# In the second feed-forward, every fourth weight unit gets its low part from an accumulating DMA instead of a subtraction

## The chip, the cores and the metric

The kernel runs on one core of one Trainium2 chip. The metric is device time in microseconds (us) of that core. The kernel before took 2350.02 us in the median of two runs (2349.10 and 2350.94). One core has a matrix engine (TensorE, PE in the profile, with its weight loads as PEld), a vector engine (VectorE, DVE), a scalar engine (ScalarE, ACT), a general engine (GpSimd, POOL), and a sync engine (SP) that in this kernel issues DMAs only. Sixteen DMA engines move data between HBM, the large memory, and SBUF, the on-chip memory of 128 partitions. TensorE adds up its products in PSUM banks.

## The reference, cut to what matters

A decoder layer on 256 tokens of width 2048 in float32: a feed-forward, a token mixer (windowed attention beside a recurrence), cross attention into a fixed memory, a second feed-forward and a last norm. The change lies in the second feed-forward, whose width is 5632:

```python
def swiglu(h, w_gate, w_up, w_down):
    return (jax.nn.silu(h @ w_gate) * (h @ w_up)) @ w_down

x = x + 0.5 * swiglu(rms_norm(x, ffn2_norm[l]), ffn2_w_gate[l], ffn2_w_up[l], ffn2_w_down[l])
return rms_norm(x, final_norm)
```

## The kernel before, in words

All products with weights follow one plan (`weight_plan`). A product takes up to 16 row chunks of 128 rows and 512 columns of a weight matrix, and both halves of the tokens; its two sums lie in two PSUM banks `acc`, of which there are three. It is worked off in **units** of two row chunks, that is 256 x 512 float32 weights, 512 KB.

float32 is had from a narrower type, float32r, with two parts: a value is a high part, rounded to float32r, plus a low part, what is left. Activations are kept as such pairs. Weights come raw and are split on the way, once a unit:

- `load` (L274): SP issues the DMA of raw weights (L287). In the feed-forwards one DMA brings two units, 1 MB, into a tile `raw2` with four buffers, up to eight units ahead of the one multiplied. SP can issue it when the unit pair that had the buffer before is read for the last time.
- `divide` (L291): ACT casts the raw unit to float32r, `hi` (L299), and DVE subtracts it from the raw weights, `lo` (L300). Both tiles have three buffers, so unit u+2 can be cast when the products of unit u-1 are done. `divide` is called two units ahead (`AHEAD`).
- `multiply` (L331): for each row chunk and each half of the tokens three products, high by high (L336), high activations by low weights (L337), low activations by high weights (L338): twelve a unit.

The order in which the program issues instructions on each engine is that of the Python calls, a little rearranged by a scheduler, and each engine works off its own queue in order. Between the products stand short steps of other work: transposes of the gated values (L347), their split, and in the second feed-forward a reload of `x` and of the last norm's gain by POOL (L1153, L1155). At the end of each of the last four down products ACT squares the result (L1165) and POOL multiplies it by the gain (L1167).

The second feed-forward has 264 units: three groups of gate and up products (8 units each) and of down products (8, 8 and 6 units each, four products a group).

Of the kernel before, what the change touches and what calls it, by code (L numbers as in the profile page):

```python
# [9 lines left out]
AF = mybir.ActivationFunctionType  # L10
# [17 lines left out]
KU = 2  # L28
# The decayed query-side factors carry 2^-40, the masks and the carried state 2^40: no product
# of a later key with an earlier query, which the masks remove, can overflow.  # L30
UP, DOWN = 2.0**40, 2.0**-40
GROUPS = ((0, 4), (4, 4), (8, 3))
N4 = 20
# Weight units whose split, and whose load, runs ahead of the one that is multiplied.
AHEAD, LOADED = 2, 4
# Products before the mixer, and before the second feed-forward.
EDGES = (34, 71)


class Act:  # L40
    """Activations with features on partitions, as two float32r parts that add up to them."""

# [8 lines left out]
class Interleave:  # L51
    """Short steps of other work, traced between the steps of the weight products."""

# [35 lines left out]
def weight_plan(a):  # L89
    """Every product with a weight matrix in its order: matrix, row chunk, chunks, column, columns."""  # L90
    w = {n: v[0] for n, v in a.items() if "_w_" in n or n.startswith("w_")}
    yield from feed_forward_plan(w["ffn1_w_gate"], w["ffn1_w_up"], w["ffn1_w_down"])
    w_in = w["w_in"]
    cols = [0, 512, ATTN_W]
    for c in cols:
        yield w_in, 0, KD, c, 512
    yield w_in, 0, KD, C_RW + 3 * RW, 288
    for h in range(2):
        yield w_in, 0, KD, C_RW + RW + h * 512, 512
    for n in range(4):  # L100
        yield w_in, 0, KD, C_GATE + n * 512, 512
        yield w["w_proj_attn"], 0, 8, n * 512, 512
    for h in range(2):
        yield w_in, 0, KD, C_RW + h * 512, 512
        yield w_in, 0, KD, C_RW + 2 * RW + h * 512, 512
    for n in range(4):
        yield w_in, 0, KD, C_GATE + D + n * 512, 512
    for n in range(4):
        yield w["w_proj_rwkv"], 0, 8, n * 512, 512
    for n in range(4):  # L110
        yield w["w_out"], 0, KD, n * 512, 512
    yield w["w_cross_kv"], 0, KD, 0, 512
    yield w["w_cross_q"], 0, KD, 0, 512
    yield w["w_cross_kv"], 0, KD, 512, 512
    for n in range(4):
        yield w["w_cross_o"], 0, 4, n * 512, 512
    yield from feed_forward_plan(w["ffn2_w_gate"], w["ffn2_w_up"], w["ffn2_w_down"])
# [3 lines left out]
def decoder_layer(ctx: ExitStack, tc: tile.TileContext, a: dict, out: bass.AP):  # L121
# [18 lines left out]
    def f32(x):  # L140
        return x.bitcast(F32)
# [17 lines left out]

# [1 line left out]
    ones = cpool.tile([P, P], F32, name="ones")  # L161
# [9 lines left out]
    select(ident[:], ones[:], [[-1, P]], ALU.is_equal, 0.0, 0, 1)  # L171
    # attention bias: [previous block | current block], rows are queries
    abias = cpool.tile([P, 2, P], F32, name="abias")
    pool.memset(abias[:], 0.0)
    select(abias[:, 0, :], abias[:, 0, :], [[1, P]], ALU.is_gt, NEG, 0, -1)
    select(abias[:, 1, :], abias[:, 1, :], [[-1, P]], ALU.is_ge, NEG, 0, 1)
    # masks with the source step on partitions and the later step along the row
    ups = cpool.tile([P, P], F32, name="ups")
# [4 lines left out]
    select(mask3[:, 2, :], ups[:], [[1, P]], ALU.is_ge, 0.0, 0, -1)  # L183
    # with the later step on partitions
    mask_l = cpool.tile([P, P], F32, name="mask_l")
# [20 lines left out]

# [1 line left out]
    def row_vectors(rows, name, queue):  # L208
        """The vectors, and what fills them once their rows are there."""
        n = len(rows)  # L210
        r = cpool.tile([n, P], F32, name=name + "_r")
        at = 0
        while at < n:
            src, lo = rows[at]
            m = 1
            while at + m < n and rows[at + m][0] is src and rows[at + m][1] == lo + m * P:
                m += 1
            queue.dma_start(
                r[at : at + m, :], src[lo : lo + m * P].rearrange("(c p) -> c p", p=P)
            )  # L220
            at += m
        v = cpool.tile([P, n], F32, name=name)

        def fill():
            t = tr()
            pe.transpose(t[:, :n], r[:], ident[:n, :n])
            return act.copy(v[:], t[:, :n])

        return v, fill
# [36 lines left out]

# [1 line left out]
    plan = list(weight_plan(a))  # L268
# [5 lines left out]
    def load(u):  # L274
        """In the feed-forwards two units at once, into the pool of that phase."""
        if u >= len(units) or u in raws:
# [14 lines left out]
    def divide(u):  # L291
        if u >= len(units) or u in parts:
            return
        n, raw = units[u][3], raws[u]
        hi = wp.tile([P, KU, n], F32R, tag="hi", name="hi")
        lo = wp.tile([P, KU, n], F32R, tag="lo", name="lo")
        for s in (slice(0, 1), slice(1, 2)) if u == 0 else (slice(0, KU),):
            with tc.issue_after(first.ins) if u < AHEAD else nullcontext():
                act.copy(hi[:, s], raw[:, s])  # L299
            dve.tensor_tensor(lo[:, s], raw[:, s], f32(hi[:, s]), ALU.subtract)  # L300
        parts[u] = hi, lo
# [10 lines left out]
    def product(x: Act, w, skew=False):  # L312
        """Rows of tokens: two [128, n] banks of x.T @ (the next columns of w)."""
        pw, _, nk, _, n = plan[at["product"]]
# [25 lines left out]
    def feat(tok, cols):  # L340
        """Token rows [128, 2, n] -> at up to two column offsets [128, 2, T] with features on
        partitions."""
        b = tr()
# [6 lines left out]
    def split(x: Act, c, n, src):  # L350
        """src (float32, PSUM or SBUF) -> chunks c to c + n of x."""
        act.copy(x.at(0, c, n), src)  # L352
        dve.tensor_tensor(x.at(1, c, n), src, f32(x.at(0, c, n)), ALU.subtract)
        x.done |= set(range(c, c + n))

# [1 line left out]
    class Norm:  # L357
# [8 lines left out]
        def block(self, n, src):  # L366
            """Steps for column block n of 512, src [128, 2, 512]; the last one ends the sums."""
            for h in range(2):
# [28 lines left out]

# [1 line left out]
    def feed_forward(sp, x, norm: Norm, wg, wu, wd, done, last=False):  # L399
# [41 lines left out]

    # ==== feed-forward 1 ====
    with tc.tile_pool(name="f1", bufs=1, reuse_waits="tile") as sp:
# [28 lines left out]

    # ==== token mixer and cross attention ====
    with tc.tile_pool(name="mx", bufs=1, reuse_waits="tile") as sp:
# [17 lines left out]

        # -- attention: a group of heads and a block of queries at a time --
        def to_features(tok, dst, name):
# [14 lines left out]
        def keys_values():  # L509
            # keys of each of the four heads on both halves of the partitions  # L510
            b = feat(tok_kv, C4[:2])
# [88 lines left out]

        # -- RWKV: columns with token shift, features on partitions --
        def shifted(tok, cols, mus, outs, name):
# [35 lines left out]
        def decay_and_rate():  # L638
# [28 lines left out]
            for h in range(2):  # L667
# [15 lines left out]
                act.activation(dec[h][:], dec[h][:], AF.Exp, scale=-DECAY)  # L683
                # decay from the middle of a chunk to each step, after that to the step before it
                ee.append(t4("ee", (P, 8, P + 1)))
# [10 lines left out]
        def removal_keys(h):  # L696
# [39 lines left out]
            pool.tensor_tensor(aa[h][:], kt[h][:], ei[:], ALU.mult)  # L736
            # products of the removal keys of later with those of earlier steps: L
            for c in range(2):
# [20 lines left out]

        # (1 - D)^-1 of the 32-step diagonal blocks, one block per partition  # L760
        def substitute():
# [27 lines left out]

        # -- the attention branch, gated --  # L790
        for n in range(4):
# [8 lines left out]

        # -- RWKV: receptances and values --
        rt, vtok, bv = [], [], []
# [15 lines left out]
        def values(h):  # L818
# [3 lines left out]
            for c in range(2):  # L822
                b = tr()
                # the recurrence keeps, and the group norm wants, values less their mean in a head
                for j in range(4):
# [16 lines left out]

        # -- RWKV: the two chunks of a pair of heads --
        xb = {}
# [121 lines left out]

        # -- group norm, bonus, gate, for two pairs --
        yr = Act([], [], 4)
# [53 lines left out]

        # -- the gate of the RWKV branch --
        for n in range(4):
# [5 lines left out]

        # -- merge and project out --
        mt = act_tiles("mt", 4)
# [38 lines left out]

        # -- cross attention --
        km, vm, qc = t4("km"), t4("vm", (P, 2, 512)), t4("qc")
# [68 lines left out]

    # ==== feed-forward 2 and the last norm ====
    with tc.tile_pool(name="f2", bufs=1, reuse_waits="tile") as sp:
# [69 lines left out]
```

## Time and profile before

| | |
|---|---|
| median of the runs | 2350.02 us (2349.10 to 2350.94) |
| span of the profiled execution | 2345.8 us; the runs' median is 4.2 us longer, what lies around the span |
| TensorE busy | 2323.1 us, 99% of the span |
| DVE, ACT, POOL busy | 1256.9, 1075.6 and 130.3 us |
| low parts on DVE (L300) | 769, 1223 ns each in the mean |
| casts on ACT (L299) | 769, 1044 ns each in the mean |
| moved by DMA | 432.71 MB, 184 GB/s over the span |
| granted clock of TensorE, mean | 0.999 |

An engine's busy time is the sum of its instructions' durations. The chain of waits is followed back from the last instruction: at each step to what released it, or to the instruction ahead of it on its engine. In a row of the timeline stand the start in us, the duration in us, engine, line, operation, output and inputs, and in brackets how long the engine was idle before it and what released it. The matmul rows overlap, as matmuls are pipelined: one is 0.39 us long, and the next starts about 0.23 us after it.

### The profile page before, as it was taken

What the parts mean: (1) busy time and instruction counts of PE and PEld (TensorE: products, weight loads), DVE (VectorE), ACT (ScalarE), POOL (GpSimd) and SP (SyncE); (2) the same over time, 40 slices, a digit from 0 to 9 for tenths busy, and PEclk for the clock granted to TensorE, in tenths of its full rate; (3) what the DMA queues carried; (4) which work ended last, traced back from release to release, by engine and by line L of the source; (5) the groups of instructions that cost most, each with busy time, mean ns of one, the idle gap of its engine ahead of it and who ended that gap; (6) DMA issues with size and microseconds to landing.
All of it is one profiled execution on the core that took longest, in us unless ns stands there. A gap on an engine that the chain in (4) does not pass through costs nothing.

```text
span 2345.8 us, 27378 instructions
## 1 busy us (share of the span) xinstructions
PE 2323.1 (99%) x10869; PEld 1897.3 (81%) x10869; DVE 1256.9 (54%) x1393; ACT 1075.6 (46%) x1425; POOL 130.3 (6%) x192
## 2 busy tenths in 40 slices
PE   8999999999999999999999999999999999999998
PEld 7888888888888877888888878888888888888886
DVE  5544444544555477795444456555545544544554
ACT  5443344433445477444344546455443344434444
POOL 1000000000000000201220030001000000000001
PEclk9999999999999999999999999999999999999999
DMA  8555556655554644676432576648555556555653
GB/s 288 182 194 183 194 185 192 190 187 188 188 188 145 177 128 146 211 224 200 118 99 84 182 246 218 192 161 290 186 193 184 187 190 195 183 190 187 197 180 126
DMA packets 219856, 432.71 MB, mean 184 GB/s; under 512 B 14267, under 2 KB 17040, under 8 KB 219728
## 3 DMA queue, kind: packets, MB, share of 16 engines
q1 hardware_dynamic: 211520, 405.58, 54.3%
q0 software_dynamic: 8176, 25.38, 3.4%
q8 instruction: 85, 1.39, 0.2%
q14 instruction: 43, 0.35, 0.0%
q10 hardware_dynamic: 32, 0.01, 0.0%
HBM read 417.56 MB, written 13.11 MB: 184 GB/s over the span
## 4 chain that ended last, share of the span: by engine, by line
PE 93%; issue 4%; DVE 1%; ACT 1%; DMA 1%; POOL 0%; SPq 0%; POOLq 0%; ACTq 0%
PE acc L336 28%; PE acc L338 28%; PE acc L337 28%; PE tr L347 2%; PE mm L925 1%; PE tr L893 1%; DMA raw<-in_ffn_w_gate_dram 0%; ACT hi L299 0%; PE mm L536 0%; POOL ml L1047 0%; PE tr L908 0%; PE tr L912 0%; PE tr L995 0%; DVE lo L300 0%; PE tr L575 0%
## 5 line engine op out<-in xcount | busy, mean ns | idle before, releaser
L300 DVE TENSOR_TENSOR lo<-raw,hi 128x1024 fp32r<-128x1024 f32 (+1 forms) x769 | 940.2, 1223 | 981.5 <-ACT hi L299 980.7
L299 ACT CAST hi<-raw 128x1024 fp32r<-128x1024 f32 (+1 forms) x769 | 802.5, 1044 | 1084.1 <-PE acc L338 1040.8
L336 PE MATMUL acc<-hi,xhi 128*128 128x512 f32 (+1 forms) x2016 | 798.6, 396 | 0.8 <-ACT xhi L373 0.5
L337 PE MATMUL acc<-lo,xhi 128*128 128x512 f32 (+1 forms) x2016 | 784.7, 389 | 0.3 <-DVE lo L300 0.3
L338 PE MATMUL acc<-hi,xlo 128*128 128x512 f32 (+1 forms) x2016 | 784.8, 389 | 0.0
L336 PEld LDWEIGHTS acc<-hi,xhi 128*128 128x128 f32 x2016 | 379.4, 188 | 81.1 <-issue 3.4
L337 PEld LDWEIGHTS acc<-lo,xhi 128*128 128x128 f32 x2016 | 379.4, 188 | 79.0 <-issue 3.3
L338 PEld LDWEIGHTS acc<-hi,xlo 128*128 128x128 f32 x2016 | 378.7, 188 | 79.3 <-issue 1.0
L336 PE MATMUL acc<-hi,hhi 128*128 128x512 f32 x704 | 280.6, 399 | 0.0
L338 PE MATMUL acc<-hi,hlo 128*128 128x512 f32 x704 | 279.1, 396 | 0.0
L337 PE MATMUL acc<-lo,hhi 128*128 128x512 f32 x704 | 279.0, 396 | 0.0
L338 PEld LDWEIGHTS acc<-hi,hlo 128*128 128x128 f32 x704 | 132.6, 188 | 32.3
L337 PEld LDWEIGHTS acc<-lo,hhi 128*128 128x128 f32 x704 | 132.7, 188 | 31.5
L336 PEld LDWEIGHTS acc<-hi,hhi 128*128 128x128 f32 x704 | 132.6, 188 | 31.4
L336 PE MATMUL acc<-hi,mthi 128*128 128x512 f32 x128 | 51.7, 404 | 0.0
L338 PE MATMUL acc<-hi,mtlo 128*128 128x512 f32 x128 | 50.6, 395 | 0.0
L337 PE MATMUL acc<-lo,mthi 128*128 128x512 f32 x128 | 50.4, 394 | 0.0
L1167 POOL TENSOR_TENSOR x<-x,fin 128x512 f32<-128x512 f32 x6 | 8.9, 1497 | 704.0 <-ACT junk L1165 704.0
L465 POOL DMA_DIRECT2D x1d<-x x4 | 3.0, 744 | 717.9 <-DVE x L427 717.9
L415 ACT ACTIVATE hb<-acc,rs 128x512 f32<-128x512 f32 x44 | 30.2, 691 | 19.6 <-PE acc L338 19.6
L352 ACT CAST hhi<-tr 128x512 fp32r<-128x512 f32 x44 | 25.7, 585 | 16.7 <-PE tr L347 16.7
L373 ACT ACTIVATE xhi<-tr,gains 128x256 fp32r<-128x256 f32 x48 | 22.0, 472 | 22.1 <-DVE xlo L374 16.2
(288 smaller groups left out, 1640.8 us busy)
## 6 DMA issues: line engine op xcount, KB each, us to landing
raw<-in_ffn_w_up_dram SPq DMA_DIRECT2D x88, 1024.0 KB, 5.2
raw<-in_ffn_w_down_dram SPq DMA_DIRECT2D x88, 1024.0 KB, 5.1
raw<-in_ffn_w_gate_dram SPq DMA_DIRECT2D x86, 1024.0 KB, 5.2
raw<-in_w_in_dram SPq DMA_DIRECT2D x136, 512.0 KB, 3.7
raw<-in_w_out_dram SPq DMA_DIRECT2D x32, 512.0 KB, 4.3
raw<-in_w_proj_attn_dram SPq DMA_DIRECT2D x16, 512.0 KB, 3.8
raw<-in_w_proj_rwkv_dram SPq DMA_DIRECT2D x16, 512.0 KB, 6.4
raw<-in_w_cross_kv_dram SPq DMA_DIRECT2D x16, 512.0 KB, 3.6
```

What stands on the lines that cost most here:

```text
L299: act.copy(hi[:, s], raw[:, s])
L300: dve.tensor_tensor(lo[:, s], raw[:, s], f32(hi[:, s]), ALU.subtract)
L336: pe.matmul(o, xh, hi[:, i, :], start=k + i == 0, stop=False)
L337: pe.matmul(o, xh, lo[:, i, :], start=False, stop=False)
L338: pe.matmul(o, xl, hi[:, i, :], start=False, stop=k + i == nk - 1)
L347: pe.transpose(b[:, o : o + P], tok[:, t, col : col + P], ident[:])
L352: act.copy(x.at(0, c, n), src)
L373: last = act.activation(self.x.at(0, c), b[:, j, :], AF.Copy, scale=g)
L415: act.activation(hb[:, t, :], pg[t][:], AF.Silu, scale=norm.r[t])
L893: pe.matmul(b[e][:, m * P : (m + 1) * P], x1[r, j, cs_], x2[r, j, cs_], start=True, stop=True,)
L925: pe.matmul(vb[:, (o + e) * P : (o + e + 1) * P], lhs(e), rhs[:], start=first and e == 0, stop=True, **ek,)
L1167: pool.tensor_tensor(xs, xs, fin[:, n * 512 : (n + 1) * 512], ALU.mult)
```

## The change

From the 41st unit of the second feed-forward on (`u >= ends[1] + 40`), every fourth unit (`u % 4 == 1`) forms its low part in another way. ACT casts the high part as before, then writes the negated high part into the low tile. POOL then issues a DMA that adds the raw weights onto that tile. Every second time the raw weights are read from HBM once more, otherwise from the raw tile in SBUF. The other units are unchanged, and the raw weights of the changed units are still loaded by SP.

```diff
             with tc.issue_after(first.ins) if u < AHEAD else nullcontext():
                 act.copy(hi[:, s], raw[:, s])
-            dve.tensor_tensor(lo[:, s], raw[:, s], f32(hi[:, s]), ALU.subtract)
+            if u >= ends[1] + 40 and u % 4 == 1:
+                act.activation(lo[:, s], f32(hi[:, s]), AF.Copy, scale=-1.0)
+                w, k, c0, _ = units[u]
+                wd = w[k * P : (k + KU) * P, c0 : c0 + n].rearrange("(a p) n -> p a n", p=P)
+                pool.dma_start(lo[:], wd if u % 8 == 1 else raw[:], accum_op=ALU.add)
+            else:
+                dve.tensor_tensor(lo[:, s], raw[:, s], f32(hi[:, s]), ALU.subtract)
         parts[u] = hi, lo
```

The rest of the diff takes out comments and adds blank lines in their places. In the changed kernel lines after the edit stand six further down: L336 to L338 become L342 to L344.

## The prediction

> **What bounds the kernel now.** I read the page's engine table and its chain of waits first, then the second feed-forward alone by windows, then who waits for whom there.
>
> ```profile
> PE 2323.1 (99%) x10869; PEld 1897.3 (81%) x10869; DVE 1256.9 (54%) x1393; ACT 1075.6 (46%) x1425; POOL 130.3 (6%) x192
> ...
> PE 93%; issue 4%; DVE 1%; ACT 1%; DMA 1%; POOL 0%; SPq 0%; POOLq 0%; ACTq 0%
> ```
>
> ```profile
> 1710.00:2285.00 575.00, 575.00 (x2545) 471.60 (x2545) 285.53 (x259) 237.29 (x242) 0.00 (x0) 1.00 0.58 189
> ```
>
> ```profile
> PE acc L337 <- DVE lo L300: 0.3, 1, 0.3
> PE acc L336 <- ACT hb L415: 0.2, 1, 0.2
> ```
>
> In the window's row the columns are PE, weight loads, DVE, ACT, POOL, then granted clock, DMA share and GB/s. TensorE is busy for all of the 575 us, at clock 1.00, in the stretch where nearly all changed units lie, and from 1600 to 2330 us its waits add up to 0.5 us. So this stage is bound by TensorE alone: work taken off DVE (285.53 of 575 us) gains nothing, and each microsecond that TensorE is made to wait is a microsecond of the total. The question is only whether the low part still comes in time.
>
> How much time it has is read from the timeline of one gate unit and one down unit.
>
> ```profile
> 1903.62 0.39 PE L338 MATMUL acc<-hi,xlo 128*128 128x512 f32 x1
> 1903.85 0.39 PE L336 MATMUL acc<-hi,xhi 128*128 128x512 f32 x1
> 1904.05 1.05 ACT L299 CAST hi<-raw 128x1024 fp32r<-128x1024 f32 x1 [1.67 <-PE acc L338]
> 1905.13 1.23 DVE L300 TENSOR_TENSOR lo<-raw,hi 128x1024 fp32r<-128x1024 f32 x1 [1.50 <-ACT hi L299]
> 1906.57 0.39 PE L336 MATMUL acc<-hi,xhi 128*128 128x512 f32 x1
> 1909.29 0.39 PE L336 MATMUL acc<-hi,xhi 128*128 128x512 f32 x1
> 1909.52 0.39 PE L337 MATMUL acc<-lo,xhi 128*128 128x512 f32 x1
> ...
> 2083.05 1.05 ACT L299 CAST hi<-raw 128x1024 fp32r<-128x1024 f32 x1 [1.76 <-PE acc L338]
> 2088.47 0.39 PE L336 MATMUL acc<-hi,hhi 128*128 128x512 f32 x1
> ```
>
> The high and low tiles have three buffers each. The last product of unit u-1 ends at 1903.62 + 0.39 = 1904.01; this frees a buffer, and 0.04 us later ACT casts unit u+2. TensorE meanwhile multiplies u (from 1903.85) and u+1 (from 1906.57), a new unit every 2.72 us, and reads u+2's low part at 1909.52. Today DVE has it ready at 1905.13 + 1.23 = 1906.36: 3.16 us to spare. That margin is all the new path can spend beyond DVE's 1.23 us.
>
> **The change, part by part.** Of the 264 units of this feed-forward the 224 after the first 40 qualify, and a quarter of them, 56, change: 34 in gate and up products, 22 in down products; 28 take the raw weights from HBM again, 28 from SBUF.
>
> *Removed:* 56 subtractions on DVE, 56 x 1.23 = 69 us of DVE time. Worth 0, as DVE was not waited for.
>
> *Added on ACT:* 56 negations of 128x1024. The nearest row is the cast of the same shape, 1.05 us; 56 x 1.05 = 59 us on an engine with 237 of 575 us busy. The cast to cast distance is 2.72 us and cast plus negation 2.10 us, so the next cast isn't late. Behind a negation at the end of a gate product queue the two reads of its banks:
>
> ```profile
> L415 ACT ACTIVATE hb<-acc,rs 128x512 f32<-128x512 f32 x44 | 30.2, 691 | 19.6 <-PE acc L338 19.6
> ```
>
> The first of them, 0.69 us, is due half a unit into the next product, when its second bank is wanted (three banks, two in use), and has been ready half a unit before the product's end: 2.72 us of room for 1.05 + 0.69. Cost 0; were that cover gone, at most 1.05 us a time.
>
> *Added on POOL:* 56 issues. POOL is idle in the window (0.00), and what else stands in its queue is clear of it:
>
> ```profile
> 1611.72 0.58 POOL L1155 DMA_DIRECT2D fin<-in_final_norm_dram  x1
> 2288.44 2.94 POOL L1167 TENSOR_TENSOR x<-x,fin 128x512 f32<-128x512 f32 x2 [676.15 <-ACT junk L1165]
> ```
>
> The reload is issued before the first changed unit, which stands 223 units of 2.72 to 2.81 us before the end of the products, that is after 1710 us; the three multiplications at the end could hold one or two of the last four issues for some tenths of a us. Cost 0.
>
> *The new wait.* Cast ends at 1905.10, negation takes 0.03 + 1.05, and POOL issues about 0.05 us later: 1906.23. In the changed program's order the scheduler has put a second high product ahead of the waiting low one in 47 of the 56 units, so the need moves from 1909.52 to 1909.75 there. The transfer thus has 3.52 us in gate and up units. In down units (cast 2083.05, need 2088.47 + 0.46) it has 3.7. Weighted, with the nine units without that step: **3.55 us from issue to landing**. Behind the waiting product stands all of TensorE's queue, so what exceeds 3.55 us is lost whole. It isn't made up: casts of u+3 and u+4 run during the stall, but u+6 again can't start before u+3's products end, so every changed unit has the same budget anew.
>
> *What the transfer takes.* No accumulating DMA is in the trace. The nearest rows are 512 KB copies issued by POOL (microseconds from issue to landing; the last row has the min/median/max of the x3d stores and reloads):
>
> ```profile
> x<-x1d POOLq DMA_DIRECT2D x4, 512.0 KB, 6.3
> ...
> x3d<-x POOLq DMA_DIRECT2D x4, 512.0 KB, 4.1
> ...
> x<-x3d POOLq DMA_DIRECT2D x4, 512.0 KB, 10.3
> ```
>
> ```profile
> DMA to landing us min/median/max: 3.3/6.0/13.2
> ```
>
> ```profile
> q1 hardware_dynamic: 211520, 405.58, 54.3%
> ```
>
> So the bounds are 3.3 us (nothing lost: 0) and 13.2 us (56 x 9.65 = 540 us). Below nothing it can't go, as TensorE had no wait to lose. Inside them I choose by source. From SBUF the nearest row is a store that reads SBUF, 4.1 us; from HBM it is a load through the same queue beside the weight stream, 6.3 us. The HBM kind meets that stream directly: the unit is the second of its pair, ACT's cast is now the last reader of the raw tile, so SP sends the next 1 MB about 1 us ahead of it. The SBUF kind holds its raw tile until it lands, so that 1 MB comes after it.
>
> ```profile
> raw<-in_ffn_w_up_dram SPq DMA_DIRECT2D x88, 1024.0 KB, 5.2
> ...
> SPq L287 <- DVE lo L300: 637.8, 126, 5.9
> ```
>
> (The 1 MB held back lands 5.2 us later and is wanted more than four units, 11 us, on: cost 0.) To either kind I add the second read that an addition needs, 0.524 MB at the rate of the weight queue, 405.58 MB in 54.3% of 2345.8 us = 318 GB/s: 1.65 us. That gives 5.75 and 7.95 us, and stalls of 2.2 and 4.4 us.
>
> On that second read: the Trainium skill, "Collectives: The Full Stack" (Part 3), says of a reducing transfer that the add costs no cycles but "needs two source reads". No run here shows it yet. "DMA: Bandwidth & Descriptors" (Anatomy of one DMA) fits a POOL-issued DMA as 2.0 us + bytes / 436 GB/s; with the bytes twice that is an estimate of 4.4 us, a stall of 0.85 us and 48 us in all, against this change far more mildly than my sum; the 6.3 us row of this trace is above what the fit has for one copy (3.2 us).
>
> **Sum:** 28 x 2.2 + 28 x 4.4 = 185 us. The profiled span is 2345.8 us; the median of the runs, 2350.02, is 4.2 us above it, which lies around the span and stays. 2350 + 185 = **2535 us**.
>
> **Rivals.**
> *Single pass.* The addition is done in flight and costs what a copy does: 4.1 and 6.3 us, stalls 0.55 and 2.75, 28 x 3.3 = 92 us, 2442 us. For it: DMA share is 0.58, there is room. Against: a copy reads once.
> *Hidden, not slower.* POOL's queue is idle and a lone transfer lands as fast as the fastest store, 3.3 us, below the 3.55 us budget; TensorE never waits, 2350 to 2360 us. It decides at a mean of 3.55 + 47 / 56 = 4.4 us: below that the loss is within 2% (47 us), which is about what a measurement of this kernel can tell from no change. Against: of the rows above only the stores are that fast, and half the units load from HBM.
> *Slow adder.* The addition runs far below copy speed, 10.3 us (the reload beside weights) or more: stalls 6.75 to 9.65, 378 to 540 us, 2728 to 2890 us. For: no row excludes it.
> *The clock.* TensorE's clock fell at the end of this run, with the last matmul's row ahead of it:
>
> ```profile
> 2336.85 0.39 PE L338 MATMUL acc<-hi,hlo 128*128 128x512 f32 x1
> ```
>
> ```profile
> 2340.00:2340.50 0.50, 0.00 (x0) 0.00 (x0) 0.50 (x2) 0.50 (x2) 0.00 (x0) 1.00 0.00 0
> 2340.50:2341.00 0.50, 0.00 (x0) 0.00 (x0) 0.48 (x1) 0.50 (x2) 0.00 (x0) 0.54 0.00 0
> ```
>
> After 2336.85 + 0.39 = 2337.24 no matmul runs, and about 3.3 us later the clock goes to half. If the 4.4 us stalls do that, and half clock lasts as long again, each costs 1.65 us more: 28 x 1.65 = 46 us, 2581 us; stalls of 2.2 us don't reach it. The Trainium skill, "TensorE: Matmul & The Clock Gate" (Part 1), has the gate close after an idle window of about 3.4 us that runs free, so only part of such stalls would span one; the 3.3 us of this trace agrees.
>
> That the change does something other than it says is no rival: the program's order has 56 negations, 56 POOL transfers into the low tile and 56 products waiting for them.
>
> **How the numbers follow.** Forecast with its own span of 2470 to 2570: 0.52. Clock rival: 0.06. Single pass: 0.18. Hidden: 0.10. Slow adder: 0.14. The range leaves out the hidden case and most of the slow adder: **2400 to 2720 us**. Slower by over 2%: all but the hidden case and a little of the single pass, 0.88; within 2%: 0.11; faster by over 2%: 0.01, as TensorE's own 575 us of 575 don't shrink.
>
> **What the profile after would show.** Right: low products (now L343) head the list of TensorE's waits with POOL's DMA named, some 56 waits and about 185 us; HBM transfers land later than SBUF ones by about 2 us; TensorE's busy time stays near 2323 us; the stretch before 1710 us is unchanged. Wrong: landings under 4.4 us on average, or over 10; waits put to ACT's casts or to raw loads, which would mean that ACT or the weight stream became late; a granted clock under 1.00 between 1710 and 2335 us.

## The result, and the profile after

The changed kernel takes 2531.68 us in the median of two runs (2539.01 and 2524.34); before, 2350.02. The ratio is 1.0772, with a 95% interval of 1.0739 to 1.0804: slower by 7.7%, and within 4 us of the forecast. The profiled execution is the one of 2539.01 us; its span is 2537.1 us, 191.3 us over the span before. The working below is against that.

The page's engine table and its chain of waits, after:

```profile
PE 2392.3 (94%) x10869; PEld 1932.5 (76%) x10869; DVE 1191.4 (47%) x1337; ACT 1133.7 (45%) x1481; POOL 190.0 (7%) x248
...
PE 78%; DMA 13%; issue 4%; ACT 4%; DVE 1%; POOL 0%; SPq 0%; POOLq 0%; ACTq 0%
```

DMA, 1% of the chain before, now holds 13%, and ACT 4%: the cast, the negation and the transfer of the changed units lie on the path. One thing doesn't fit waits alone: TensorE does the same 10869 matmuls and is *busy* for 69.2 us longer (2392.3 against 2323.1).

Who waits for whom on TensorE (total us, times, longest us):

```profile
PE acc L343 <- DMA lo<-in_ffn_w_down_dram: 35.0, 11, 3.5
PE acc L343 <- DMA lo<-raw: 32.8, 28, 2.0
PE acc L343 <- DMA lo<-in_ffn_w_up_dram: 31.0, 9, 4.4
PE acc L343 <- DMA lo<-in_ffn_w_gate_dram: 22.5, 8, 3.4
```

56 waits, one for each changed unit, 121.3 us in all: 1.17 us each for the SBUF kind (32.8 / 28), 3.16 for the HBM kind (88.5 / 28). The transfers behind them, KB each and the median us from issue to landing, in the DMA view between 1700 and 2480 us (53 of the 56):

```profile
lo<-raw POOLq DMA_DIRECT2D x26, 512.0 KB, 4.6
lo<-in_ffn_w_down_dram POOLq DMA_DIRECT2D x10, 512.0 KB, 7.0
lo<-in_ffn_w_up_dram POOLq DMA_DIRECT2D x9, 512.0 KB, 6.8
lo<-in_ffn_w_gate_dram POOLq DMA_DIRECT2D x8, 512.0 KB, 6.7
```

The other 70 us are seen in the timeline of a unit of each kind, the SBUF kind first:

```profile
1906.75 0.63 PE L342 MATMUL acc<-hi,hhi 128*128 128x512 f32 x2
1908.39 0.51 PE L343 MATMUL acc<-lo,hhi 128*128 128x512 f32 x1 [1.01 <-DMA lo<-raw]
1908.74 0.39 PE L344 MATMUL acc<-hi,hlo 128*128 128x512 f32 x1
...
1916.28 1.20 POOL L304 DMA_DIRECT2D lo<-in_ffn_w_gate_dram  x1 [11.61 <-ACT lo L301]
...
1919.20 0.61 PE L342 MATMUL acc<-hi,xhi 128*128 128x512 f32 x2
1922.63 0.52 PE L343 MATMUL acc<-lo,xhi 128*128 128x512 f32 x1 [2.82 <-DMA lo<-in_ffn_w_gate_dram]
...
1923.80 0.63 PE L343 MATMUL acc<-lo,xhi 128*128 128x512 f32 x1
...
1924.65 0.63 PE L343 MATMUL acc<-lo,xhi 128*128 128x512 f32 x1
...
1925.93 0.60 PE L343 MATMUL acc<-lo,xhi 128*128 128x512 f32 x1
...
1926.84 0.40 PE L343 MATMUL acc<-lo,xhi 128*128 128x512 f32 x1
```

and in the windows around the second (length, then PE, PEld, DVE, ACT, POOL, granted clock, DMA share, GB/s):

```profile
1919.57:1922.98 3.41, 0.59 (x4) 0.31 (x3) 1.23 (x1) 0.87 (x1) 0.00 (x0) 1.00 0.81 145
1922.98:1926.40 3.42, 3.42 (x10) 2.68 (x9) 0.00 (x0) 0.00 (x0) 0.00 (x0) 0.50 0.85 298
```

*Restarting.* Without the wait the low product would have followed at about 1907.21, 0.23 us after the second high one. It starts at 1908.39, 1.18 us late, though the row says 1.01 (the wait is counted from the modelled end of the product before it), and the next product comes 0.35 us after it instead of 0.23. A stall thus costs about 0.29 us beyond its row: 56 x 0.29 = 16 us. (The 34 stalls of this trace that have no half clock next to them give 0.28 in the mean.)

*The clock.* After the HBM stall matmuls take 0.63 us instead of 0.39 for 3.4 us, and the granted clock there is 0.50. In the trace's clock records it falls to half, here called a closing, 26 times in the changed stretch, 25 times after a stall of the HBM kind and once after a long one of the SBUF kind (2.03 us), for 3.4 or 6.8 us each. Over 1710 to 2470 us the mean is 0.93:

```profile
1710.00:2470.00 760.00, 646.55 (x2588) 510.30 (x2587) 229.94 (x211) 296.91 (x303) 57.99 (x54) 0.93 0.62 181
```

The records of that stretch add up to 119.5 us at half clock, so at most half of that, 60 us, is lost. What is left of the span, 191.3 - 121.3 - 16 = 54 us, is the clock's by this reckoning, 2.1 a closing. It is a remainder, and the span before is itself known to a few us only: in the runs before that stand beside the experiments it lies between 2345.5 and 2352.1 us.

### The profile page after: what moved, and what is told of

Read it like the earlier page. It is cut to its first block, busy times and chain, and to the rows that moved or that the text cites. A ratio compares the mean times of both kernels' runs of the same rounds, so it can differ in the third digit from the quotient of the medians.

```text
span 2537.1 us, 27614 instructions
## 1 busy us (share of the span) xinstructions
PE 2392.3 (94%) x10869; PEld 1932.5 (76%) x10869; DVE 1191.4 (47%) x1337; ACT 1133.7 (45%) x1481; POOL 190.0 (7%) x248
## 4 chain that ended last, share of the span: by engine, by line
PE 78%; DMA 13%; issue 4%; ACT 4%; DVE 1%; POOL 0%; SPq 0%; POOLq 0%; ACTq 0%
PE acc L343 24%; PE acc L344 23%; PE acc L342 23%; DMA lo<-raw 5%; DMA lo<-in_ffn_w_down_dram 3%; DMA lo<-in_ffn_w_up_dram 2%; DMA lo<-in_ffn_w_gate_dram 2%; ACT hi L299 2%; PE tr L353 2%; ACT lo L301 1%; PE mm L931 1%; PE tr L899 1%; DMA raw<-in_ffn_w_gate_dram 0%; PE mm L542 0%; POOL ml L1053 0%
## 5 line engine op out<-in xcount | busy, mean ns | idle before, releaser
L306 DVE TENSOR_TENSOR lo<-raw,hi 128x1024 fp32r<-128x1024 f32 (+1 forms) x713 | 871.0, 1222 | 1184.3 <-ACT hi L299 1183.6
L343 PE MATMUL acc<-lo,xhi 128*128 128x512 f32 (+1 forms) x2016 | 805.1, 399 | 75.6 <-DMA lo<-in_ffn_w_up_dram 31.0
L342 PE MATMUL acc<-hi,xhi 128*128 128x512 f32 (+1 forms) x2016 | 805.8, 402 | 1.3 <-ACT xhi L379 1.0
L344 PE MATMUL acc<-hi,xlo 128*128 128x512 f32 (+1 forms) x2016 | 800.3, 397 | 0.0
L343 PEld LDWEIGHTS acc<-lo,xhi 128*128 128x128 f32 x2016 | 388.9, 193 | 170.5 <-DMA lo<-in_ffn_w_up_dram 34.8
L342 PEld LDWEIGHTS acc<-hi,xhi 128*128 128x128 f32 x2016 | 386.9, 192 | 84.9 <-issue 3.6
L344 PEld LDWEIGHTS acc<-hi,xlo 128*128 128x128 f32 x2016 | 388.4, 193 | 82.1 <-issue 1.3
L343 PE MATMUL acc<-lo,hhi 128*128 128x512 f32 x704 | 288.6, 410 | 46.1 <-DMA lo<-in_ffn_w_down_dram 35.0
L344 PE MATMUL acc<-hi,hlo 128*128 128x512 f32 x704 | 285.8, 406 | 0.0
L342 PE MATMUL acc<-hi,hhi 128*128 128x512 f32 x704 | 282.5, 406 | 0.0
L344 PEld LDWEIGHTS acc<-hi,hlo 128*128 128x128 f32 x704 | 137.1, 195 | 32.6
L342 PEld LDWEIGHTS acc<-hi,hhi 128*128 128x128 f32 x704 | 136.2, 194 | 32.7
L301 ACT ACTIVATE lo<-hi 128x1024 fp32r<-128x1024 f32 x56 | 59.4, 1061 | 1.8
L304 POOL DMA_DIRECT2D lo<-raw x28 | 25.5, 911 | 416.1 <-ACT lo L301 385.4
L342 PE MATMUL acc<-hi,mthi 128*128 128x512 f32 x128 | 51.8, 404 | 0.0
L344 PE MATMUL acc<-hi,mtlo 128*128 128x512 f32 x128 | 50.5, 395 | 0.0
L433 DVE SCALAR_TENSOR_TENSOR x<-acc,x 128x512 f32<-128x512 f32 x48 | 32.0, 686 | 32.7 <-PE acc L344 32.7
L424 DVE SCALAR_TENSOR_TENSOR hb<-acc,rs,hb 128x512 f32<-128x512 f32 x44 | 31.8, 746 | 20.5 <-PE acc L344 20.5
```

The costliest lines, as they stand in the source:

```text
L301: act.activation(lo[:, s], f32(hi[:, s]), AF.Copy, scale=-1.0)
L304: pool.dma_start(lo[:], wd if u % 8 == 1 else raw[:], accum_op=ALU.add)
L342: pe.matmul(o, xh, hi[:, i, :], start=k + i == 0, stop=False)
L343: pe.matmul(o, xh, lo[:, i, :], start=False, stop=False)
L344: pe.matmul(o, xl, hi[:, i, :], start=False, stop=k + i == nk - 1)
L424: dve.scalar_tensor_tensor(hb[:, t, :], pu[t][:], norm.r[t], hb[:, t, :], ALU.mult, ALU.mult)
```

## The experiments

The first four ran on one chip, the last four together in a second job, each beside runs of the kernel before (medians 2350.95 and 2350.80 us, all between 2347.2 and 2353.9). The kernel with filled stalls was timed four times and the split two units earlier ten times; every other time is that of one run.

**One kind of source alone.** All transfers from SBUF:

```diff
-                pool.dma_start(lo[:], wd if u % 8 == 1 else raw[:], accum_op=ALU.add)
+                pool.dma_start(lo[:], raw[:], accum_op=ALU.add)
```

> All 56 transfers read the raw tile in SBUF. In the changed kernel the SBUF kind made TensorE wait 32.8 us over 28 units, 1.17 each, and the clock was half only after HBM stalls. Theory (the clock falls only after the long stalls of the HBM kind): 56 x 1.17 = 66 us of waits, granted clock 1.00 in the second feed-forward, 2350 + 66 = 2416 us. Rival (the clock loss of 69 us belongs to any stall, half to each kind): 2350 + 66 + 69 = 2485 us.

Measured: 2430.1 us. The wait on TensorE and the window 1710 to 2280 us:

```profile
PE acc L343 <- DMA lo<-raw: 59.9, 56, 2.7
```

```profile
1710.00:2280.00 570.00, 520.39 (x2228) 412.72 (x2227) 197.34 (x180) 253.98 (x257) 38.61 (x45) 0.99 0.69 209
```

Stalls of 1.07 us in the mean leave the clock at 0.99. The rival's 2485 us is out; the theory is 14 us short, most of which the restart explains: 59.9 + 56 x 0.29 = 76 us, and two closings of the clock, after the two longest waits in the stretch (2.02 and 2.69 us), come to about 3 more. The span grew by 82.5 us over the 2345.8 of the profile before, and the time by 79 us over the median of the runs beside it.

All from HBM:

```diff
-                pool.dma_start(lo[:], wd if u % 8 == 1 else raw[:], accum_op=ALU.add)
+                pool.dma_start(lo[:], wd, accum_op=ALU.add)
```

> All 56 transfers read HBM again. The HBM kind made TensorE wait 88.5 us over 28 units, 3.16 each. Theory (the clock loss is the HBM kind's alone, 69 / 28 = 2.47 us a stall): 56 x (3.16 + 2.47) = 315 us, 2665 us. Rival (loss spread over both kinds alike, 1.23 a stall): 56 x (3.16 + 1.23) = 246 us, 2596 us.

Measured: 2619.85 us, between the two and nearer the rival, yet for another reason.

```profile
PE acc L343 <- DMA lo<-in_ffn_w_down_dram: 69.5, 22, 3.6
PE acc L343 <- DMA lo<-in_ffn_w_up_dram: 61.5, 18, 4.2
PE acc L343 <- DMA lo<-in_ffn_w_gate_dram: 47.4, 16, 3.4
```

```profile
1710.00:2280.00 570.00, 457.89 (x1750) 359.56 (x1749) 155.16 (x143) 200.54 (x203) 43.01 (x36) 0.89 0.59 164
```

The waits are 178.4 us, 3.19 each, as the theory had them; the clock's mean is 0.89. The span grew by 272.3 us; less 178.4 and 16 for restarts, the clock cost 78 us, 1.4 a stall. The 2.47 us that the theory gave each stall had the restarts in it, and not every stall closes the clock: 40 closings for 56 stalls.

**The addition left out.**

```diff
-                pool.dma_start(lo[:], wd if u % 8 == 1 else raw[:], accum_op=ALU.add)
+                pool.dma_start(lo[:], wd if u % 8 == 1 else raw[:])
```

> The same 56 transfers without the addition: the low tile is overwritten with the raw weights, so the addition is left out and the output is not the layer's. Theory of the prediction (an addition costs a second read, 1.65 us): landings fall from 4.6 and 6.8 us to about 3.0 and 5.2, SBUF stalls vanish, HBM stalls are 1.6 us, 28 x 1.6 = 45 us, 2395 us. Rival (the second read runs beside the first and is free): landings and time as with the addition, 4.6 and 6.8 us, 2532 us.

Measured: 2421.68 us. The landings are the theory's, 2.9 and 5.2 to 5.5 us:

```profile
lo<-raw POOLq DMA_DIRECT2D x28, 512.0 KB, 2.9
lo<-in_ffn_w_down_dram POOLq DMA_DIRECT2D x11, 512.0 KB, 5.5
lo<-in_ffn_w_up_dram POOLq DMA_DIRECT2D x9, 512.0 KB, 5.3
lo<-in_ffn_w_gate_dram POOLq DMA_DIRECT2D x8, 512.0 KB, 5.2
```

So the addition costs 1.7 us from SBUF (4.6 - 2.9) and about 1.5 from HBM (6.8 - 5.3). It isn't all a second read: POOL's issue itself grew from 0.57 to 0.91 us and from 0.70 to 1.20, which is a fifth to a third of it. The rest shows in the DMA engines. POOL's queue moves the same packets and bytes between 1700 and 2600 us here and, with the addition, in the kernel with filled stalls below:

```profile
q0 software_dynamic: 11648, 29.36, 9.9%
q0 software_dynamic: 11648, 29.36, 18.1%
```

The share is that of 16 engines' time, so each of the 56 transfers takes them 900 x 8.2% / 56 = 1.3 us longer. That this is a second read isn't shown: the bytes counted stay the same.

The time is 27 us above the theory, which had left out the restarts and eight closings of the clock, after HBM stalls of 1.85 to 2.74 us (1.75 in the mean of all 28).

**The stall filled with matmuls.** This tests the clock with the transfers as they are:

```diff
             u = next_unit()
+            v = at["unit"] - 1
+            if v >= ends[1] + 40 and v % 8 == 1:
+                d = mm()
+                for _ in range(10):
+                    pe.matmul(d[:], x.at(0, k)[:, 0:P], u[0][:, 0, :], start=True, stop=True)
             for t in range(2):
```

> Ten matmuls of the unit's high part into an unused PSUM bank stand ahead of the 28 units that wait for an HBM transfer; nobody reads them. They take 10 x 0.227 = 2.3 us of stalls that are 3.2 us long, so the end of each wait stays where it is. Theory (idle TensorE lets the clock go to half, which costs the 69 us by which TensorE's busy time grew): clock 1.00 in the second feed-forward, 2532 - 69 = 2463 us. Rival (the clock is not lost by idling, or matmuls were slow for another reason): no gain, 2532 us or more.

Measured: 2494.48 us, ratio to before 1.0613 (1.0595 to 1.0631); the changed kernel's 1.0772 (1.0739 to 1.0804) lies clear above. 280 matmuls more make the kernel 37 us faster. The window 1710 to 2280 us:

```profile
1710.00:2280.00 570.00, 523.51 (x2247) 415.60 (x2246) 179.48 (x164) 232.88 (x234) 44.46 (x42) 1.00 0.66 190
```

The clock's mean is 1.00: it closes twice in the whole changed stretch instead of 26 times, after an HBM wait of 1.93 us and an SBUF wait of 2.04. So idling does lose it, and the loss is real. The gain is 37 us and not 69: the 69 us of busy time held the restarts' slow first matmuls too, and the filled stalls came out a little longer than the empty ones (27.8 us still waited and 28 x 2.27 = 63.6 us filled, 91.4 against 88.5). Between the two profiled spans, 2537.1 and 2491.5, the difference is 46 us; so the clock's share of the changed kernel is some 40 to 55 us, not settled closer than its two runs, 15 us apart, allow. Their mean granted clocks, 0.974 and 0.980, account for that distance: 0.026 x 2537 = 66 us of clock missing in the first, 0.020 x 2523 = 50 in the second.

**The negation alone.** ACT negates, DVE subtracts as before:

```diff
                 act.activation(lo[:, s], f32(hi[:, s]), AF.Copy, scale=-1.0)
-                w, k, c0, _ = units[u]
-                wd = w[k * P : (k + KU) * P, c0 : c0 + n].rearrange("(a p) n -> p a n", p=P)
-                pool.dma_start(lo[:], wd if u % 8 == 1 else raw[:], accum_op=ALU.add)
+                dve.tensor_tensor(lo[:, s], raw[:, s], f32(hi[:, s]), ALU.subtract)
```

> ACT writes the 56 negated high parts as in the changed kernel, but DVE then forms the low part by subtraction as before; no accumulating DMA. Theory (ACT has room): TensorE waits for nothing, 2350 us. Rival (1.06 us more on ACT delays casts or the reads of the banks): up to 56 x 1.06 = 59 us, 2409 us.

Measured: 2350.22 us. In its window of 1710 to 2280 us TensorE is busy for 570.00 of 570 us with ACT at 288.32, against 235.19 before. ACT's part costs nothing that one run can tell.

**The HBM transfer without the weight stream ahead of it.**

```diff
+    held = cpool.tile([P, 1], F32, name="held")
...
                 pool.dma_start(lo[:], wd if u % 8 == 1 else raw[:], accum_op=ALU.add)
+                if u % 8 == 1:
+                    pool.tensor_tensor(held[:], raw[:, 0, 0:1], f32(lo[:, 0, 0:1]), ALU.add)
```

> After each of the 28 HBM transfers POOL reads one column of the low and of the raw tile, so the raw tile stays taken until the transfer has landed and SP's next 1 MB cannot start ahead of it. Theory (the HBM kind is slow because it shares the DMA engines with that 1 MB): landing falls from 6.8 to about 5.3 us, stalls from 3.2 to 1.7 us, the clock stays, 28 x (1.7 + 1.17) = 80 us, 2430 us. Rival (reading HBM is itself what takes longer): landing 6.8 us, 2532 us.

Measured: 2484.75 us, between the two; the theory's 5.3 us of landing and its unchanged clock both missed.

```profile
lo<-raw POOLq DMA_DIRECT2D x28, 512.0 KB, 4.5
lo<-in_ffn_w_down_dram POOLq DMA_DIRECT2D x11, 512.0 KB, 6.2
lo<-in_ffn_w_up_dram POOLq DMA_DIRECT2D x9, 512.0 KB, 5.9
lo<-in_ffn_w_gate_dram POOLq DMA_DIRECT2D x8, 512.0 KB, 6.0
```

With the 1 MB held back, no weight packets to speak of move during the transfer (0.01 us of the 16 engines' time in the mean, against 3.1 in the changed kernel), and it lands in 6.0 us instead of 6.8, so the collision costs 0.8 of the 2.2 us between the kinds. The remaining 1.5 us over the SBUF kind stay; 0.3 of them are the longer issue, 1.20 against 0.91 us. Whether the rest is the HBM read or the 2 KB rows (the SBUF kind moves 4 KB rows) was not tried. The HBM waits fell to 67.3 us and the clock closed 14 times instead of 25, which is the larger part of the gain of 47 us; the waits' own is 21.

**The split begun earlier.** The changed units have two high and two low tiles of their own and are split one unit ahead of the others, or two (`changed(u)` is the condition `u >= ends[1] + 40 and u % 4 == 1`; the code is that of two units):

```diff
-        hi = wp.tile([P, KU, n], F32R, tag="hi", name="hi")
-        lo = wp.tile([P, KU, n], F32R, tag="lo", name="lo")
+        if changed(u):
+            hi, lo = (
+                at["pool"].tile([P, KU, n], F32R, tag=m + "2", name=m, bufs=2)
+                for m in ("hi", "lo")
+            )
+        else:
+            hi = wp.tile([P, KU, n], F32R, tag="hi", name="hi")
+            lo = wp.tile([P, KU, n], F32R, tag="lo", name="lo")
...
-            if v <= u + AHEAD:
+            if v <= u + AHEAD + (2 if changed(v) else 0):
```

> The 56 changed units are split one unit earlier, into two high and two low tiles of their own; all else as changed. Budget of the transfer 3.55 + 2.75 = 6.3 us. Theory (the cost is lateness alone): the SBUF kind (4.6 us) is hidden, the HBM kind (6.8) stalls 0.5 us, 28 x 0.5 = 14 us, clock 1.00, 2364 us. Rival (the added DMA traffic or ports slow the rest): over 2400 us.

> As early1, but two units earlier: budget 9 us. Theory (lateness alone): both kinds hidden, TensorE waits for nothing, 2350 us. Rival (the traffic itself costs): over 2400 us.

Measured: 2353.97 us one unit earlier, and 2352.01 us two units earlier, ratio 1.0012 (1.0003 to 1.0022). One unit earlier the 14 us of HBM waits that the theory still had did not come: the HBM transfers landed in 5.9 to 6.6 us there, in the medians by matrix. Who waits on TensorE from 1600 to 2330 us, and the window 1710 to 2280 us, two units earlier:

```profile
PE acc L352 <- DVE lo L315: 0.5, 2, 0.2
PE acc L351 <- ACT hb L430: 0.3, 1, 0.3
```

```profile
1710.00:2280.00 570.00, 570.00 (x2513) 465.30 (x2512) 220.60 (x205) 287.48 (x290) 53.74 (x51) 1.00 0.82 236
```

The same 56 accumulating transfers, DMA share up from 0.58 to 0.82, DVE relieved by 63 us in this window (283.70 before, 220.60 now), and TensorE waits 0.8 us in all. So the loss is lateness alone, not traffic; and the DVE time set free is worth nothing, as no wait for it was there to remove. No version faster than before came of it.

## Why the prediction was right

**The mechanism held.** TensorE alone bounds the stage, the freed DVE time gains nothing, and ACT's negations are hidden (2350.22 us with them alone). The transfer has about 3.55 us, and the excess is paid in full at every changed unit: 4.6 - 3.55 = 1.05 and 6.8 - 3.55 = 3.25, measured waits 1.17 and 3.16. The two-kind split by source, 2.2 us apart, was forecast and seen, though the meeting with the weight stream, which the forecast named for the HBM kind, makes only 0.8 of it. The stretch up to 1600 us is unchanged, with TensorE busy for 1586.40 us before and 1585.83 after.

**The sum came out through two errors that cancel; that it is right to 4 us is luck.** The step "what the transfer takes" was too dear by 1.15 us a unit: it started from 4.1 us (a store to HBM) and 6.3 us (loads beside the weights), and a copy of each kind measured 2.9 and 5.3. The 1.65 us put on top for the addition was right (1.7 and 1.5), though part of it is POOL's issue and not a read. So the waits are 121.3 us and not 185, 64 us less.

What filled the gap are two terms that the sum lacked: the restarts, about 16 us, and the clock, some 40 to 55 us. The clock stood among the rivals with a chance of 0.06, and there with the wrong threshold: "stalls of 2.2 us don't reach it" and 3.3 us of idleness as the price of entry were read off one drop at the end of the program, with TensorE idle throughout. It closes at waits of 1.85 us and up, by where they fall (last section), and the test "granted clock under 1.00" that the prediction set itself as a sign of error did come true (0.93). TensorE's busy time, forecast near 2323 us, rose to 2392.3.

**Of the rivals**, *hidden* failed on the landings: even the SBUF kind, at 4.6 us, is above 4.4. *Single pass* is refuted by the run without the addition, where a copy lands 1.5 to 1.7 us sooner, and not by the landings of the changed kernel: 4.6 and 6.8 us lie nearer to its 4.1 and 6.3 than to the forecast's 5.75 and 7.95, and the waits, 121.3 us, nearer to its 92 than to 185. *Slow adder* failed too: the longest landing is 7.7 us, not 10.3. On the Trainium skill's "DMA: Bandwidth & Descriptors" (Anatomy of one DMA), whose fit with the bytes twice gave an estimate of 4.4 us: the SBUF kind measured 4.6, close to it, the HBM kind 6.8, well above. The Trainium skill's "Collectives: The Full Stack" (Part 3) has a reducing transfer's addition cost a second source read; the 1.5 to 1.7 us agree in size with one more read at 318 GB/s (1.65 us), but 0.3 to 0.5 of them are the longer issue, and no count of bytes here shows the read.

## What to carry to other kernels

Where one engine bounds a stage, moving work off another engine gains nothing, and the question is only whether the new path is shorter than the time between a buffer's release and its use; count that time in the timeline, and give a longer path earlier starts and buffers of its own before anything else. For the length of a transfer take the row with the same source, destination and queue neighbours, not the nearest in size. A stall of TensorE costs more than its row: a restart each time (0.29 us here), and from about 2 us on often the clock as well.

## What the runs showed of the hardware that had not been expected

The clock doesn't need a whole idle window. The Trainium skill, "TensorE: Matmul & The Clock Gate" (Part 1), has it close after an idle window of about 3.4 us. The half-clock stretches here do come in lengths of 3.4 and 6.8 us, but the window ahead of the one shown above held 0.59 us of matmuls in 3.41, and waits far shorter than a window closed the clock too, down to one of 1.85 us. By the traces' clock records, in the changed stretch:

| kernel | mean wait of the stalls, us | closings / such stalls | waits that closed it, us |
|---|---|---|---|
| all from SBUF | 1.07 | 2 / 56 | 2.02 and 2.69 |
| addition left out, HBM kind | 1.75 | 8 / 28 | 1.85 to 2.74 |
| HBM kind held clear of the stream | 2.40 | 14 / 28 | 1.93 to 2.71 |
| changed kernel, HBM kind | 3.16 | 25 / 28 | 2.41 to 4.37 |
| all from HBM | 3.19 | 40 / 56 | 2.31 to 4.15 |

The wait alone doesn't decide. In each trace all closings of the stretch begin on one grid of 3.413 us, and what a window of that grid holds of matmul time tells whether the clock falls at its end. Take all windows of the changed stretch that ran at full clock, in these five kernels and the one with filled stalls. The 92 after which the clock fell held 1.57 us or less, by the matmul rows; the 1171 after which it stayed held 1.48 or more. The same wait therefore costs a closing or not by where it falls. In the changed kernel an HBM wait of 3.40 us lay across two windows and left 1.69 and 1.74 us of matmuls in them; the clock stayed. The SBUF wait of 2.03 us lay inside one window and left 1.38; the clock fell:

```profile
2062.91:2066.32 3.41, 1.69 (x8) 1.07 (x6) 2.28 (x2) 1.23 (x2) 0.00 (x0) 1.00 1.09 271
2066.32:2069.74 3.42, 1.74 (x7) 1.42 (x8) 0.17 (x1) 0.00 (x0) 0.00 (x0) 1.00 0.74 198
2069.74:2073.15 3.41, 3.41 (x16) 2.82 (x15) 1.22 (x1) 1.05 (x1) 0.00 (x0) 1.00 0.36 138
...
2428.14:2431.55 3.41, 1.38 (x7) 0.82 (x5) 1.71 (x2) 1.05 (x1) 0.00 (x0) 1.00 0.81 154
2431.55:2434.97 3.42, 3.42 (x8) 2.72 (x9) 0.00 (x0) 0.00 (x0) 0.00 (x0) 0.50 0.63 192
```

Whether the limit, about 1.5 us in 3.41, is the same for other matmuls than these was not measured.
